# Giving ScalarE one row's sum of the first tile, in a kernel that divides rows by the sum of their absolute values

## Chip, cores, metric

One core of one Trainium2 chip. The metric is the device time of one execution in microseconds (us), median of the runs named. A span is the same execution as the trace sees it, 1.6 to 1.8 us shorter than the device time. VectorE and ScalarE are the two engines that compute here; SyncE only issues transfers. The DMA engines do the copying between the chip's main memory and the tile buffers, and take their work from queues. Tiles and loads are counted from 0.

## The reference

```python
# x: (32, 512, 1024) float32
sums = np.sum(np.abs(x), axis=-1, keepdims=True)
return (x / (sums + 1e-8)).astype(np.float32)
```

That is 16384 rows of 1024 numbers: 67.1 MB are read and as many written, in float32, and nothing in the problem allows less.

## The kernel before

The rows are cut into eleven tiles: ten of 128 partitions x 12 rows (6.29 MB each), and a last one of 8 rows (4.19 MB). Four buffers hold tiles. For each tile SyncE issues the load, VectorE sums the absolute values of all rows, adds epsilon and takes the reciprocal, VectorE and ScalarE share the multiplication by rows, and ScalarE's queue issues the store. The load of tile i+4 has to wait until the store of tile i has landed, because they share a buffer.

```python
R = 12; BUFS = 4
... # rows = [12]*10 + [8]; piece(flat, i) is the part of x or out of tile i
def normalize(x_tile, r0, k, kv):
    s = stats.tile([P, R], FP32)
    nc.vector.tensor_reduce(out=s[:, :k], in_=x_tile[:, r0 : r0 + k, :],
        axis=mybir.AxisListType.X, op=mybir.AluOpType.add, apply_absolute_value=True)
    nc.vector.tensor_scalar_add(out=s[:, :k], in0=s[:, :k], scalar1=EPS)
    inv = stats.tile([P, R], FP32)
    nc.vector.reciprocal(out=inv[:, :k], in_=s[:, :k])
    nc.vector.tensor_mul(out=x_tile[:, r0 : r0 + kv, :], ...)        # kv rows on VectorE
    for r in range(kv, k):                                           # the rest on ScalarE
        nc.scalar.activation(out=row, in_=row, func=...Copy, scale=inv[:, r : r + 1])

for i, k in enumerate(rows):
    x_tile = sbuf.tile([P, R, d], FP32)
    nc.sync.dma_start(out=x_tile[:, :k, :], in_=piece(x_flat, i))
    normalize(x_tile, 0, k, k - k // 3 - (i == 0))
    nc.scalar.dma_start(out=piece(out_flat, i), in_=x_tile[:, :k, :])
```

## Time and profile before

| | before |
|---|---|
| device time, 3 runs | 317.16 us (316.67 to 318.14) |
| span of the profiled run | 315.5 us |
| moved by DMA | 134.2 MB, 425 GB/s over the span |
| VectorE, ScalarE busy | 74%, 15% of the span |
| last load used from, last store issued | 280.36 us, 296.24 us |

How to read it: at the steady rate of 434 GB/s (the prediction shows the row) the bytes alone need 134.2 / 0.434 = 309.2 us of the 315.5. The table says at once that VectorE is the busiest compute engine.

### The profile page before, as it was taken

How to read it: one execution, taken by the hardware profiler on the slowest of the kernel's cores; microseconds unless marked ns; L12 is line 12 of the kernel's file. 1: busy time of each engine (PE TensorE's matmuls, PEld its weight loads, DVE VectorE, ACT ScalarE, POOL GpSimd, SP SyncE). 2: the span in 40 equal slices, each digit the busy share in tenths (PEclk: the TensorE clock that was granted, in tenths of full speed). 3: DMA queues.
4: the chain of work that ended last, by engine and by line, in shares of the span. 5: the costliest groups of instructions: out<-in, count | busy, mean ns of one | idle time of the engine just before them, and what ended most of it. 6: DMA issues, size and time to landing. Idle time of an engine off the chain costs nothing.

```text
span 315.5 us, 206 instructions
## 1 busy us (share of the span) xinstructions
DVE 234.7 (74%) x44; ACT 47.2 (15%) x44; POOL 0.2 (0%) x4
## 2 busy tenths in 40 slices
DVE  0079999999999399929955992899199659979500
ACT  0010603105005001300500050013004000502000
POOL 0000000000000000000000000000000000000000
DMA  8999999999999999999999999999999999999996
GB/s 330 467 399 430 467 343 455 399 467 430 399 467 430 399 486 411 405 486 405 424 474 399 436 461 399 467 430 399 467 425 405 474 403 459 407 472 411 424 432 274
DMA packets 3169, 134.23 MB, mean 425 GB/s; under 512 B 352, under 2 KB 352, under 8 KB 352
## 3 DMA queue, kind: packets, MB, share of 16 engines
q1 hardware_dynamic: 1584, 67.11, 49.8%
q10 hardware_dynamic: 1584, 67.11, 49.1%
q14 instruction: 1, 0.01, 0.0%
HBM read 67.11 MB, written 67.11 MB: 425 GB/s over the span
## 4 chain that ended last, share of the span: by engine, by line
another core or an unknown queue 36%; DMA 31%; DVE 26%; SPq 0%; issue 0%; DVEq 0%; ACTq 0%
DMA x_tile<-in_x_dram 16%; DMA out_dram<-x_tile 15%; DVE s L51 15%; DVE x_tile L61 10%; SPq L78 0%; DVE inv L60 0%; DVE s L58 0%; DVEq L60 0%; ACTq L81 0%
## 5 line engine op out<-in xcount | busy, mean ns | idle before, releaser
L51 DVE TENSOR_REDUCE s<-x_tile 128x12 f32<-128x12288 f32 (+1 forms) x11 | 138.2, 12563 | 59.8 <-DMA x_tile<-in_x_dram 59.8
L61 DVE TENSOR_TENSOR x_tile<-x_tile,inv 128x8192 f32<-128x8192 f32 (+2 forms) x11 | 92.4, 8401 | 0.4
L68 ACT ACTIVATE x_tile<-x_tile,inv 128x1024 f32<-128x1024 f32 x43 | 45.9, 1136 | 226.9 <-DVE inv L60 226.9
L68 ACT ACT_TABLE_LOAD x1 | 1.3, 1283 | 17.7 <-DMA x_tile<-in_x_dram 17.7
L60 DVE RECIPROCAL inv<-s 128x12 f32<-128x12 f32 (+1 forms) x11 | 2.5, 226 | 0.9
L58 DVE TENSOR_SCALAR s<-s 128x12 f32<-128x12 f32 (+1 forms) x11 | 1.9, 173 | 0.4
L96 POOL MEMSET const-bfloat16-1.0<- 128x1 bf16 x1 | 0.1, 102 | 0.0
L96 POOL MEMSET const-uint8-127<- 128x1 uint8 x1 | 0.1, 102 | 0.0
L96 POOL MEMSET const-float32-0.0<- 128x1 f32 x1 | 0.1, 99 | 0.2 <-issue 0.2
L96 POOL MEMSET const-float32-1.0<- 128x1 f32 x1 | 0.1, 99 | 0.0
## 6 DMA issues: line engine op xcount, KB each, us to landing
x_tile<-in_x_dram SPq DMA_DIRECT2D x10, 6144.0 KB, 37.6
out_dram<-x_tile ACTq DMA_DIRECT2D x10, 6144.0 KB, 50.7
x_tile<-in_x_dram SPq DMA_DIRECT2D x1, 4096.0 KB, 32.3
out_dram<-x_tile ACTq DMA_DIRECT2D x1, 4096.0 KB, 18.2
```

The source lines that it names most:

```text
L51: nc.vector.tensor_reduce(out=s[:, :k], in_=x_tile[:, r0 : r0 + k, :], axis=mybir.AxisListType.X, op=mybir.AluOpType.add, apply_absolute_v ...
L58: nc.vector.tensor_scalar_add(out=s[:, :k], in0=s[:, :k], scalar1=EPS)
L60: nc.vector.reciprocal(out=inv[:, :k], in_=s[:, :k])
L61: nc.vector.tensor_mul(out=x_tile[:, r0 : r0 + kv, :], in0=x_tile[:, r0 : r0 + kv, :], in1=inv[:, :kv].unsqueeze(2).to_broadcast([P, kv, d]),)
L68: nc.scalar.activation(out=row, in_=row, func=mybir.ActivationFunctionType.Copy, scale=inv[:, r : r + 1],)
L96: nc = _bacc.Bacc("TRN2", target_bir_lowering=False, num_devices=1)
```

## The change

Its intent: shorten the way to the first store. Until the first tile is done, ScalarE has nothing to do, so it takes over the sum of one of the twelve rows (absolute value with an accumulated sum; the elementwise result goes to a scratch tile in PSUM, another memory on the chip, that nobody reads).

```diff
+    junk = psum.tile([P, d], FP32)
-    def normalize(x_tile, r0, k, kv):
+    def normalize(x_tile, k, ks, kv):
         nc.vector.tensor_reduce(
-            out=s[:, :k],
-            in_=x_tile[:, r0 : r0 + k, :],
+            out=s[:, :ks],
+            in_=x_tile[:, :ks, :],
             ...
+        for r in range(ks, k):
+            nc.scalar.activation(
+                out=junk[:, :],
+                in_=x_tile[:, r, :],
+                func=mybir.ActivationFunctionType.Abs,
+                accum_out=s[:, r : r + 1],
+            )
         ...
-            normalize(x_tile, 0, k, k - k // 3 - (i == 0))
+            if i == 0:
+                normalize(x_tile, k, k - 1, k - 5)
+            else:
+                normalize(x_tile, k, k, k - k // 3)
```

Cut: the creation of the PSUM pool, and index changes where r0, always 0, falls away.

More of the change, by code (lines that the diff above doesn't have):

```diff
@@ L46 @@
     stats = ctx.enter_context(tc.tile_pool(name="stats", bufs=4))
-    def normalize(x_tile, r0, k, kv):
+    psum = ctx.enter_context(
+        tc.tile_pool(name="psum", bufs=1, space=bass.MemoryType.PSUM)
+    )
+    junk = psum.tile([P, d], FP32)
+    def normalize(x_tile, k, ks, kv):
         s = stats.tile([P, R], FP32)
         nc.vector.tensor_reduce(
-            out=s[:, :k],
-            in_=x_tile[:, r0 : r0 + k, :],
+            out=s[:, :ks],
+            in_=x_tile[:, :ks, :],
             axis=mybir.AxisListType.X,
@@ L57, in normalize @@
         )
+        for r in range(ks, k):
[4 more added lines that the diff above has]
+                accum_out=s[:, r : r + 1],
+            )
         nc.vector.tensor_scalar_add(out=s[:, :k], in0=s[:, :k], scalar1=EPS)
@@ L61, in normalize @@
         nc.vector.tensor_mul(
-            out=x_tile[:, r0 : r0 + kv, :],
-            in0=x_tile[:, r0 : r0 + kv, :],
+            out=x_tile[:, :kv, :],
+            in0=x_tile[:, :kv, :],
             in1=inv[:, :kv].unsqueeze(2).to_broadcast([P, kv, d]),
@@ L66, in normalize @@
         for r in range(kv, k):
-            row = x_tile[:, r0 + r, :]
+            row = x_tile[:, r, :]
             nc.scalar.activation(
```

## The prediction

> **What bounds the kernel now.** I read the slices of the page first, then the windows table cut at the changes of stage, then the waits of VectorE, and last the timeline of the first tile, because that is where the edit is.
>
> ```profile
> DMA  8999999999999999999999999999999999999996
> HBM read 67.11 MB, written 67.11 MB: 425 GB/s over the span
> ```
>
> The DMA engines are at 90% or more in 38 of 40 slices; only the first and the last have room. VectorE is busy for 74% and ScalarE for 15%. So the question is not how busy VectorE is but whether the DMA queues ever run dry because VectorE is late. The windows table answers by stage (columns: stretch, its length, busy time of VectorE, ScalarE and GpSimd, granted clock, DMA share, GB/s):
>
> ```profile
> 4.00:38.80 34.80, 21.04 (x5) 6.59 (x6) 0.00 (x0) 1.00 1.01 436
> 38.80:80.00 41.20, 40.99 (x8) 8.53 (x8) 0.00 (x0) 1.00 1.02 427
> 80.00:110.00 30.00, 24.82 (x5) 4.27 (x4) 0.00 (x0) 1.00 0.99 428
> 110.00:139.00 29.00, 22.05 (x4) 4.26 (x4) 0.00 (x0) 1.00 1.00 434
> 280.30:296.20 15.90, 15.62 (x4) 2.19 (x2) 0.00 (x0) 1.00 0.96 417
> 296.20:313.50 17.30, 0.00 (x0) 0.00 (x0) 0.00 (x0) 1.00 0.95 410
> ```
>
> From 4.0 to 38.8 us there are loads alone, then loads and stores together, and after 280.3 us (the last load has landed) stores alone. Loads alone already move 436 GB/s, the mixture 427 to 434, stores alone 410 to 417. A steady tile is 29.00 us long, which is 2 x 6.29 MB at 434 GB/s, while VectorE needs 22.05 us of it. In the query of the queues between 110 and 255 us the load queue and the store queue hold 50.1% each: when both have work they share equally, some 217 GB/s each.
>
> VectorE's waits say when it is ahead of the transfers and when behind:
>
> ```profile
> DVE s L51 <- DMA x_tile<-in_x_dram: 59.8, 8, 17.7
> ```
>
> Eight of eleven reduces waited for their load: the first (17.7 us), then none until the fifth tile (6.3 us), and some 6.8 us in each tile after. Tiles 1 to 3 run back to back on VectorE, from 38.66 to 105 us, and there alone could time saved on VectorE move anything. The edit is in the tile before them:
>
> ```profile
> 17.66 12.95 DVE L51 TENSOR_REDUCE s<-x_tile 128x12 f32<-128x12288 f32 x1 [17.66 <-DMA x_tile<-in_x_dram]
> 17.71 1.28 ACT L68 ACT_TABLE_LOAD   x1 [17.71 <-DMA x_tile<-in_x_dram]
> 30.65 0.18 DVE L58 TENSOR_SCALAR s<-s 128x12 f32<-128x12 f32 x1
> 30.86 0.23 DVE L60 RECIPROCAL inv<-s 128x12 f32<-128x12 f32 x1
> 31.12 5.30 ACT L68 ACTIVATE x_tile<-x_tile,inv 128x1024 f32<-128x1024 f32 x5 [12.13 <-DVE inv L60]
> 31.12 7.62 DVE L61 TENSOR_TENSOR x_tile<-x_tile,inv 128x7168 f32<-128x7168 f32 x1
> 38.66 12.94 DVE L51 TENSOR_REDUCE s<-x_tile 128x12 f32<-128x12288 f32 x1
> 38.83 0.37 ACTq L81 DMA_DIRECT2D out_dram<-x_tile  x1
> ```
>
> ScalarE loads its table at 17.71, is done at 18.99 and then stands idle for 12.13 us until the reciprocal. That hole is where the change puts its sum.
>
> **What the Trainium skill says.** "Perfetto Trace Analysis", section Roofline, gives about 435 GB/s as what one core's 16 DMA engines can pull together. The 434 GB/s of the steady stretch agrees: there is nothing left to win in it. "DMA: Bandwidth & Descriptors", section Queues, rings and completion order, says each DMA engine goes round robin, packet by packet, between the queues with work; the 50.1% and 50.1% agree. "ScalarE: Activation LUTs", section Table sets: the hidden batching unit, lists cheap functions such as copy and abs as filler in every set, so abs followed by copy should need one table load, and section What ACT_TABLE_LOAD costs puts the load at about 1283 ns; the trace has one of 1.28 us. Whether abs shares copy's set no trace of the kernel before can show.
>
> **The change, part by part.** Only tile 0 differs. The argument list loses an offset that was always 0. The split of the multiplication stays: before, 12 - 4 - 1 = 7 rows on VectorE and 5 on ScalarE; after, k - 5 = 7 and 5.
>
> Removed: one row of VectorE's first reduce. A reduce of 12 rows takes 12.95 us and of 8 rows 8.69 us, so a row is (12.95 - 8.69) / 4 = 1.065 us and the fixed part 0.17 us. Eleven rows come to 0.17 + 11 x 1.065 = 11.88 us, 1.07 us less. If it starts at 17.66 as before, it ends at 29.54 rather than 30.61.
>
> Added: one 128x1024 ScalarE activation with abs, and the output of its accumulator. The 128x1024 activations here have a mean of 1.136 us; with a short second instruction for the accumulator I estimate 1.1 to 1.4 us. It follows the table load, at 18.99, and ends near 20.4, some 9 us before VectorE is through its eleven rows. Both write parts of one statistics tile, and both read one data tile. The two multiplications of this kernel already write parts of one tile at the same time (both start at 31.12), so the dependence is kept by region and the two sums should not wait for each other. The unneeded output goes to a scratch tile in PSUM that nobody else uses.
>
> Added: a wait of VectorE's small addition for ScalarE's sum. It has long been met; where later tiles wait on a second engine, the gap between the small addition's start and the reciprocal's is 0.28 us (124.16 to 124.44) in place of 0.21 (30.65 to 30.86), so I allow 0.07 us.
>
> Sum on VectorE: 1.07 - 0.07 = 1.0 us earlier. The reciprocal begins near 29.8, the multiplication near 30.1, the second reduce near 37.6, and the first store is issued near 37.8 in place of 38.83.
>
> **What that does to the end.** The queue does not stand idle before that first store: loads 1 to 3 are still on their way at 436 GB/s. An earlier store therefore takes half the rate from the loads. In the 1.0 us by which it starts sooner the loads lose 1.0 x 217 GB/s = 0.22 MB, which costs them another 1.0 us at their half rate. So every store moves 1.0 us forward and every load 1.0 us back.
>
> The first load to matter is the fourth. It is issued near 2.3 us (the last of four that take from 0.73 to 2.65) and takes the longest time to landing of any, 80.1 us, so it lands near 82.4; VectorE gets to it at 82.78, with 0.4 us to spare. After the change VectorE is there near 81.8 and the load near 83.4. The saving ends there: tile 3 should show a new wait of about 1.6 us and begin some 0.6 us later than before. From then on VectorE waits for loads in every tile, as before.
>
> At the end: the last load lands near 281.4 in place of 280.34, the last reduce, multiplication and store follow with the same 15.9 us, and the last store is issued near 297.2 in place of 296.24. Has it room? Before, 17.3 us of stores alone at 410 GB/s are 7.1 MB, of which the last store is 4.19 MB, so 2.9 MB or 7.1 us of older stores lay in front of it. Losing 1.0 us of these 7 leaves the queue full. The end is when all 134.2 MB have been moved. What remains is a change of mixture: the stretch with stores alone gets about 1 us shorter and is 4 to 5% slower than the mixed one (413 against 434), which is worth 0.05 us. The predicted time is 317.16 - 0.05, say 317.1 us.
>
> **The rivals.** *The gain comes through whole:* a microsecond on the only back-to-back stretch of VectorE, carried to the end, would give 316.1 us. For it speaks that the chain of waits runs through VectorE from 17.66 to 82.89 us. Against it, the chain then passes into transfers of a queue that never empties, and the fourth load has only 0.4 us of slack. Even this is 0.3%.
>
> *The sums wait for each other:* if the shared statistics tile makes ScalarE's sum follow VectorE's reduce, tile 0 takes about 0.2 us more than before (1.2 added, 1.07 saved, a further hand-over) and the time is still 317.2. The simultaneous writes at 31.12 speak against it.
>
> *A second table load:* if abs and copy lie in different sets, 1.28 us come either into the idle hole (free) or between the reciprocal and the five copies; these would end at 1.28 + 5.30 = 6.6 us, still before VectorE's 7.62. Nothing is lost: 317.1.
>
> *The order of transfers:* stores begin earlier and meet other packets; the stretch 38.8 to 110 us runs at 427 to 428 GB/s, 1.5% below the steady 434, so about 71 x 0.015 = 1.1 us is lost there. A different phase could win back or double a part of it: 316.5 to 317.9. This is the only way I see to a shift above noise, and I can't tell its sign.
>
> **Range and chances.** All rivals lie between 316.1 and 317.9. The three runs of before lie between 316.67 and 318.14, so the median of a few runs has about half a microsecond of noise of its own. I take 316.2 to 318.0 for 8 in 10. A shift of 2% is 6.3 us, more than everything this change touches, so I give 98% to the same time and 1% to either side; these are for a surprise in the DMA rate.
>
> **What would show it.** Right: a first reduce of 128x11264 taking 11.9 us; an activation into the junk tile between 19 and 21 us, beside it; one table load; the first store near 37.8; a wait of VectorE for a load before the fourth reduce, which was not there; later reduces about 1 us later than before, the last store issued near 297; 434 GB/s in the steady tiles. Wrong: if later reduces start 1 us earlier and the end too (the loads didn't pay for the store), if ScalarE's sum starts after the reduce has ended, or if the steady tile is no longer 29.0 us.

## The result, and the profile after

317.25 us (317.09 to 317.71, 6 runs) against 317.32 us (316.67 to 318.14, 6 runs). The ratio is 0.9997 with a 95% interval of [0.9982, 1.0013]: the same. Here and below a ratio is the mean time of one kernel's fast runs over the mean of the other's fast runs of the same rounds, so it is not quite the ratio of the medians quoted.

The timeline of the first tile after the change (start us, length us, engine, line, operation; in brackets the idle time before and what ended it):

```profile
0.72 1.28 ACT L65 ACT_TABLE_LOAD   x1 [0.72 <-PEq L112]
...
17.75 1.03 ACT L65 ACTIVATE junk<-x_tile 128x1024 f32<-128x1024 f32 x1 [15.75 <-DMA x_tile<-in_x_dram]
17.75 11.89 DVE L57 TENSOR_REDUCE s<-x_tile 128x11 f32<-128x11264 f32 x1 [17.75 <-DMA x_tile<-in_x_dram]
18.72 0.19 ACT L65 ACTIVATION_READ_ACCUMULATOR junk<-x_tile 128x1 f32 x1
29.75 0.17 DVE L71 TENSOR_SCALAR s<-s 128x12 f32<-128x12 f32 x1
29.96 0.23 DVE L73 RECIPROCAL inv<-s 128x12 f32<-128x12 f32 x1
30.22 7.63 DVE L74 TENSOR_TENSOR x_tile<-x_tile,inv 128x7168 f32<-128x7168 f32 x1
...
37.77 12.95 DVE L57 TENSOR_REDUCE s<-x_tile 128x12 f32<-128x12288 f32 x1
37.94 0.37 ACTq L97 DMA_DIRECT2D out_dram<-x_tile  x1
```

The edit does what it was made for. ScalarE's sum lies wholly beside VectorE's shorter reduce, and the first store is issued at 37.94 us in place of 38.83. Further lines of the timelines show where this ends: at the fourth reduce. Before, then after:

```profile
82.78 12.95 DVE L51 TENSOR_REDUCE s<-x_tile 128x12 f32<-128x12288 f32 x1
```

```profile
82.05 0.34 ACTq L97 DMA_DIRECT2D out_dram<-x_tile  x1
82.77 12.95 DVE L57 TENSOR_REDUCE s<-x_tile 128x12 f32<-128x12288 f32 x1 [0.80 <-DMA x_tile<-in_x_dram]
```

The fourth reduce began at 82.78 before; it begins at 82.77 now, after a new wait of 0.80 us for its load. VectorE had finished the tile before it 0.9 us sooner (at 81.96 in place of 82.86) and stood idle for nearly all of that. VectorE's waits in total, after:

```profile
DVE s L57 <- DMA x_tile<-in_x_dram: 61.8, 9, 17.8
```

Nine waits in place of eight, and 61.8 us in place of 59.8. The 2.0 us more are about the 1.06 us of work that was taken away and the 1.06 us by which, as the next lines show, the last reduce begins later. And at the other end of the kernel, first before, then after:

```profile
280.36 8.69 DVE L51 TENSOR_REDUCE s<-x_tile 128x8 f32<-128x8192 f32 x1 [1.96 <-DMA x_tile<-in_x_dram]
...
296.24 0.34 ACTq L81 DMA_DIRECT2D out_dram<-x_tile  x1
```

```profile
281.42 8.69 DVE L57 TENSOR_REDUCE s<-x_tile 128x8 f32<-128x8192 f32 x1 [1.96 <-DMA x_tile<-in_x_dram]
...
297.29 0.34 ACTq L97 DMA_DIRECT2D out_dram<-x_tile  x1
```

The first store moved 0.89 us forward, and the last load and the last store moved 1.06 and 1.05 us BACK, while the device time stayed. This is what a fixed rate shared by two queues would look like: what the stores get sooner, the loads get later. One pair of traces does not prove it, however. The slower last tile, below, runs the program of before up to its last tile, and its last load was used at 280.75 us, 0.39 us later than in the trace of before. So some of the 1.06 us may be the run and not the change; the five-row kernel, below, shows the same shift at 4.4 us.

### The profile page after: what moved, and what is told of

Its sections match the earlier page's. It is cut to its first block, busy times and chain, and to the rows that moved or that the text cites. A ratio compares the mean times of both kernels' runs of the same rounds, so it can differ in the third digit from the quotient of the medians.

```text
span 315.9 us, 208 instructions
## 1 busy us (share of the span) xinstructions
DVE 233.8 (74%) x44; ACT 48.3 (15%) x46; POOL 0.2 (0%) x4
## 4 chain that ended last, share of the span: by engine, by line
another core or an unknown queue 36%; DMA 32%; DVE 25%; SPq 0%; issue 0%; DVEq 0%; ACTq 0%
DMA x_tile<-in_x_dram 16%; DMA out_dram<-x_tile 15%; DVE s L57 15%; DVE x_tile L74 10%; SPq L91 0%; DVE inv L73 0%; DVE s L71 0%; DVEq L73 0%; DVEq L71 0%; ACTq L97 0%
## 5 line engine op out<-in xcount | busy, mean ns | idle before, releaser
L57 DVE TENSOR_REDUCE s<-x_tile 128x12 f32<-128x12288 f32 (+2 forms) x11 | 137.1, 12467 | 61.8 <-DMA x_tile<-in_x_dram 61.8
L65 ACT ACTIVATE junk<-x_tile 128x1024 f32<-128x1024 f32 x1 | 1.0, 1027 | 15.7 <-DMA x_tile<-in_x_dram 15.7
```

What stands on the lines that cost most here:

```text
L57: nc.vector.tensor_reduce(out=s[:, :ks], in_=x_tile[:, :ks, :], axis=mybir.AxisListType.X, op=mybir.AluOpType.add, apply_absolute_value=True,)
L65: nc.scalar.activation(out=junk[:, :], in_=x_tile[:, r, :], func=mybir.ActivationFunctionType.Abs, accum_out=s[:, r : r + 1],)
```

## The experiments

Theory: the end is pinned by the bytes; a head start of VectorE in the first tile only shifts turns between the load and the store queue. Rivals: (A) the head start is carried to the end but one microsecond is lost in noise; (B) the new sum costs as much as it saves; (C) some computing elsewhere is on the path, and only the place of the edit was wrong. Rival B needs no run of its own: the trace above has the sum beside the reduce, and the store 0.89 us sooner. All of these ran with correct results unless said otherwise.

**Five rows instead of one.** From the changed kernel:

```diff
-                normalize(x_tile, k, k - 1, k - 5)
+                normalize(x_tile, k, k - 5, k - 5)
```

> ScalarE sums five rows of tile 0 and VectorE seven. Theory (an earlier store is paid for by the loads, the end is pinned by the bytes): the first reduce takes 0.17 + 7 x 1.065 = 7.6 us, ScalarE's five sums some 5.5 us beside it, the first store is issued near 33.7 us (5.2 us before that of the kernel before), the last reduce starts 5.2 us LATER than before, near 285.5, the last store near 301.4, time 317.0 us, within 0.5 us of before. The room before the last store shrinks from 7 to about 2 us but stays positive. Rival (a head start of VectorE is carried to the end, one microsecond was only lost in noise): 5 us off, 312 us, and the last reduce starts near 275.

318.01 us (317.45 to 320.95, 6 runs) against 317.50 (11 runs); ratio 1.0021 [0.9977, 1.0066]. The timeline of its first store, of the third and fourth reduces and of its end:

```profile
33.63 0.38 ACTq L97 DMA_DIRECT2D out_dram<-x_tile  x1
...
57.25 12.95 DVE L57 TENSOR_REDUCE s<-x_tile 128x12 f32<-128x12288 f32 x1 [1.65 <-DMA x_tile<-in_x_dram]
86.26 12.95 DVE L57 TENSOR_REDUCE s<-x_tile 128x12 f32<-128x12288 f32 x1 [6.86 <-DMA x_tile<-in_x_dram]
...
284.79 8.69 DVE L57 TENSOR_REDUCE s<-x_tile 128x8 f32<-128x8192 f32 x1 [1.94 <-DMA x_tile<-in_x_dram]
...
300.67 0.34 ACTq L97 DMA_DIRECT2D out_dram<-x_tile  x1
```

The first store leaves 5.2 us sooner than in the kernel before (33.63 against 38.83), the fourth reduce begins 3.5 us LATER (86.26 against 82.78) and the last 4.4 us later; I had expected 5.2. The time does not fall. Rival A wanted 312 us and falls.

**A slower first tile.** The kernel before, with one more reduce of the tile in tile 0, its result unused:

```diff
+        for _ in range(extra):                     # extra = 1 for tile 0, else 0
+            t = spare.tile([P, R], FP32)
+            nc.vector.tensor_reduce(out=t[:, :k], in_=x_tile[:, r0 : r0 + k, :], ...)
```

> The kernel before with one more reduce of 12 rows (12.95 us) in tile 0, its result unused. Theory: the stores start 13 us later, near 51.8, the loads get ahead; the store queue is never empty afterwards, so the DMA engines stay full; the last reduce starts EARLIER than before, between 267 and 276 us; the stretch with stores alone gets longer and is 4 to 5% slower, worth 0.3 to 0.7 us; time 317.2 to 318.2 us. Rival (the chain of waits through VectorE in the first 83 us sets the end): 330 us. Rival (half of it shows): about 323.

319.91 us median, but its runs are wide: 317.35 to 324.69, two of six slow; ratio of the fast runs 1.004 [0.999, 1.009]. Against the 13 us added this is nothing or at most about 3 us; the interval can't say whether the small loss is real. The profiled run, at 317.35, is the fastest of the six, and its span is 315.6 us against 315.5; its trace can't say what the slower runs lost. The windows table of this run shows that in it the DMA engines did not notice (same columns as in the prediction):

```profile
38.80:80.00 41.20, 40.99 (x9) 9.57 (x9) 0.00 (x0) 1.00 1.01 422
80.00:110.00 30.00, 29.79 (x8) 5.26 (x5) 0.00 (x0) 1.00 1.00 429
110.00:139.00 29.00, 28.82 (x5) 7.53 (x8) 0.00 (x0) 1.00 1.00 434
```

VectorE is busy without a gap here (29.79 of 30 us), and the rates are within 1.2% of those of the kernel before, 427, 428 and 434. My number for the last reduce was wrong: I said 267 to 276 us, it began at 279.25, only 1.1 us earlier than before. The queues say why. Between 66 and 80 us of this run:

```profile
q10 hardware_dynamic: 138, 6.00, 99.0%
q1 hardware_dynamic: 16, 0.00, 0.1%
```

The load queue (q1) moved nothing: all four buffers were full, and the next load could be issued only when the first store had landed, at 77.18 us. Meanwhile the stores (q10) had the engines to themselves, at 428 GB/s, and made up what they had lost. The load of tile 5 is then issued at 102.55 us, against 102.58 in the kernel before. So the lead of the loads over the stores is capped by the buffers, and a delay of 13 us is forgotten within two tiles.

**A slower last tile.** The same extra reduce, twice, in the last tile instead (extra = 2 for tile 10).

> The kernel before with two more reduces of 8 rows (17.4 us) in the LAST tile, results unused. Theory: older stores hide about 7 us of it, the rest shows: last store issued near 313.6, time 317.2 + 17.4 - 7.1 = 327.5 us (326.5 to 328.5). Rival (VectorE is nowhere on the path, as the busy shares suggest): 317. Rival (the tail has no room at all): 334.6.

328.60 us (328.32 to 329.25, 4 runs); ratio 1.0346 [1.0301, 1.0392], slower, 11.1 us over the median of before and 1.1 us above my point, just outside the range I gave. The windows table of the end:

```profile
296.20:303.00 6.80, 6.80 (x2) 0.00 (x0) 0.00 (x0) 1.00 1.05 455
303.00:313.60 10.60, 10.43 (x4) 2.19 (x2) 0.00 (x0) 1.00 0.01 5
313.60:325.00 11.40, 0.12 (x1) 0.00 (x0) 0.00 (x0) 1.00 0.86 369
```

This is what it looks like when VectorE is on the path: at 303 us the older stores are through, and the engines stand at 5 GB/s for 10.6 us until the last store is issued at 313.81. The last store came 313.81 - 296.24 = 17.6 us later and the span grew by 326.8 - 315.5 = 11.3 us, so older stores hid 6.3 us; I had worked out 7.1. So it is the place of the work, and not the share of busy time, that decides whether it shows: 13 us added in the first tile showed next to nothing, 17.4 us in the last showed 11.

**No computing at all.** WRONG ON PURPOSE: the call of normalize is left out, tiles are stored as loaded.

```diff
-            normalize(x_tile, 0, k, k - k // 3 - (i == 0))
```

> WRONG ON PURPOSE: the tiles are stored as they were loaded, no computing at all, same tiles, buffers and queues. Theory (bytes pin the time): about 2 us of start, 134.2 MB at about 434 GB/s, about 2 us to land the last store, and a shorter stretch of stores alone: 315 to 317 us, so all the computing costs about 1 us. Rival (computing on the path, which a better split could win back by more than 2%): under 311 us.

316.99 us (316.60 to 317.86, 6 runs) against 317.50; ratio 0.9982 [0.9942, 1.0022]. The page of this run:

```profile
span 315.2 us, 80 instructions
...
DMA  8989999999999999999999999999999999999997
```

A copy through the same tiles takes as long as the kernel, within the interval. In the two profiled runs all computing together costs 0.3 us of span (315.5 against 315.2), less than the spans of the copy differ among themselves (314.8 to 316.1). With this, rival C falls too: as far as the copy is the floor, no other split of the work between the engines can win more than the interval leaves, 0.6%, with these tiles and queues. That the copy is the floor is argued: it moves the same bytes, but in another order in time, its first store being issued at 17.63 us.

**Small pieces at both ends.** A try for a version that beats both: pieces of 4, ten times 12, and 4 rows; VectorE sums all. From the changed kernel; cut: the bounds of the pieces, and the call for tile 0, which becomes `normalize(x_tile, k, k, k - 1)`.

```diff
-    HEAD = 32
+    HEAD = 8
-    rows = [R] * ((per_partition - HEAD) // R + 2) + [HEAD - 2 * R]
+    rows = [HEAD // 2] + [R] * ((per_partition - HEAD) // R) + [HEAD // 2]
```

> Pieces of 4, ten times 12, and 4 rows in place of 12 (ten times) and 8; VectorE sums all. The first store can be issued near 15 us, so the loads lead by 13 us in place of 36 and the stretch with stores alone shrinks from 33 us to about 15. Theory: only the 4 to 5% slower rate of stores alone can be won back, 18 us x 0.045 = 0.8 us: 316.5 us, not below the copy without computing (317.0) by more than its noise, so 316.0 to 317.5. Rival (the long stretches of one direction are a real loss of several us, which an earlier first store would cure): 312 to 314. Rival (so small a lead lets a queue run dry): over 319, with waits in the profile.

317.72 us (317.04 to 317.89, 6 runs) against 317.55; ratio 0.9995 [0.9960, 1.0029]. The first store is issued at 16.31 us, 22.5 us sooner than before, and nothing comes of it. The expected 0.8 us did not appear either; from 15 to 60 us, when stores had joined the loads, this kernel moved only 417 GB/s, and from 298 to 314 us only 379. So what the mixture could give was lost there or was never there; no run separates the two.

**Three buffers.** Does the same hold when buffers are scarce? The kernel before, the changed kernel and the five-row kernel, each with `BUFS = 3`, the first two in two sessions.

> The kernel before with three buffers in place of four. A load is issued when the store of the tile three before it has landed. Theory: the load queue runs dry for some us in each tile while stores keep the engines busy, 318 to 326 us; DMA share mostly still 0.9 or more.

> The changed kernel with three buffers. Theory: as the kernel before with three buffers, within 1 us (first store 0.9 to 1.0 us earlier, not carried to the end, as the transfers bind still). Rival (it is the fourth buffer that swallowed the microsecond): 1 us faster than the three-buffer kernel before, with every reduce 1 us earlier to the last.

> The kernel before with three buffers, a second time, as the partner of the next two: 330 to 333 us in its fast runs.

> The changed kernel with three buffers, a second time, since three of its four runs were slow. If the microsecond is carried through with three buffers, its profile shows later reduces about 1.2 us earlier than those of the three-buffer kernel before, as in the first pair, and its fast runs are about 1 us shorter; if that was chance, the sign differs this time.

> Five rows summed by ScalarE in tile 0, three buffers: first store 5.1 us earlier. If three buffers let a head start through: the last reduce about 5 us earlier, and about 326 us. If the bytes bind here too: the time of the three-buffer kernel before within 1.5 us.

| three buffers | all runs, us | fast runs of these | ratio to the four-buffer kernel before |
|---|---|---|---|
| before, first session | 330.39 to 335.33 | 4 of 4 | 1.0469 [1.0398, 1.0540] |
| changed, first session | 330.28 to 338.51 | 1 of 4 | none |
| before, second session | 324.31 to 337.88 | 1 of 6 | none |
| changed, second session | 330.53 to 337.67 | 5 of 6 | 1.0481 [1.0417, 1.0545] |
| five rows, second session | 328.70 to 336.10 | 5 of 6 | 1.0427 [1.0365, 1.0489] |

Two things follow. Three buffers cost about 4 to 5%, more than the 318 to 326 us that I had expected: the reduces wait for loads by up to 14 us. And the comparison is not settled. In the first session's profiled runs every later reduce of the changed kernel is 1.1 to 2.5 us earlier (the last at 300.24 against 301.52) and the span is 1.3 us shorter (328.1 against 329.4), which would suit the rival that the fourth buffer swallows the microsecond. But runs of one and the same three-buffer kernel differ by 5 to 14 us, and a run is marked slow when it is over 1.5% above the fastest of its kernel, so one lucky run (324.31) turns all the others slow. In the second session the profiled runs of two of the three kernels were slow, so I compare no traces there. The ratios of the changed and the five-row kernel overlap with that of the kernel before. With three buffers the question whether a head start is carried through stays open.

## Why the prediction was right

**The time and the bound.** Predicted 317.1 us, measured 317.25. The 0.05 us that the mixture was to give is far below the noise and is not shown. "There is nothing left to win" in the steady stretch was the load-bearing step. The steady tiles still move 434 GB/s after the change, and the copy without computing takes 316.99 us, the kernel's time within the interval. One line was misread on the way: the waits after the fifth tile are not all some 6.8 us, the last was 1.96 us. Nothing rests on it.

**The price of the sum.** Predicted 11.88 us for the reduce of eleven rows, measured 11.89; predicted 1.1 to 1.4 us for ScalarE's sum, measured 1.03 + 0.19 with a small overlap. The two sums did not wait for each other, and there was one table load, so abs and copy did share a set. One step had the wrong place: I put the sum after the table load, at 18.99 us. The table load began at 0.72 us, where the kernel before had it wait for the tile (why it no longer waits, the trace does not show), and the sum began with the reduce at 17.75. It changed nothing, since ScalarE's sum ended over 10 us before VectorE's.

**The first store.** Predicted 37.8 us, measured 37.94. The difference is that the first tile's load was used 0.09 us later than before. The 0.07 us allowed for the second wait came as predicted, but before the small addition (0.11 us after the reduce's end in place of 0.04), not after it.

**The loads pay.** Predicted: every store about 1.0 us sooner and every load about 1.0 us later, with a last reduce near 281.4 and a last store near 297.2. Measured: 281.42 and 297.29. The direction is right, and the five rows confirm it. That the last reduce agrees to less than a tenth is in part luck, since two traces of what is up to there the same program differ by 0.39 us, and the steps on the way were not 1.0. The load of tile 4 waits for the first store to land; its issue, before, then after:

```profile
73.52 0.33 SPq L78 DMA_DIRECT2D x_tile<-in_x_dram  x1
```

```profile
71.75 0.33 SPq L91 DMA_DIRECT2D x_tile<-in_x_dram  x1
```

So the first store landed 1.8 us sooner. The fourth load took 80.6 us to landing in place of 80.1, only 0.5 us longer, so the fourth reduce waited 0.80 us and not the predicted 1.6. The next ones began 0.59 us later (111.76 against 111.17), then 0.82, 0.82, 1.22, 1.09, 1.06 and 1.06.

The term that was mis-sized is the exchange at the first store. The working had the store take half of the rate as soon as it is issued. But in both kernels the store queue moved nothing before 43 us, with the store issued at 38.83 us before and at 37.94 after. From 43 to 73 us the two queues shared equally in the kernel before:

```profile
q1 hardware_dynamic: 149, 6.54, 51.2%
q10 hardware_dynamic: 150, 6.64, 51.1%
```

After the change the stores had more in the same stretch, 6.93 MB against 6.29 MB of loads. So the earlier issue did not bring the store's first bytes forward; it got the stores a larger part of what followed. Why a store that is issued behind loads waits 4 us and more, and why the turns then fell as they did, no run here shows.

**The tail.** I took about 7 us of older stores as the room before the last store; the slower last tile measured 6.3. The change took 1.05 us of that room.

## What to carry to other kernels

When the DMA engines are full from the first load to the last store, time saved on a compute engine is first turned into idle time of that engine, and an earlier store is paid for by later loads; check the last load and the last store, not only the first. A kernel stripped of its computing gives an estimate of the floor in one run, and it should come before any rebalancing of engines. Where work can still matter is the stretch after the last load: there the room is what older stores leave in the queue, here 6 us, and of a delay of 17.6 us the other 11.3 showed.

## What the Trainium skill lacked or had wrong

- "DMA: Bandwidth & Descriptors", section Where 436 GB/s comes from, says that for transfers between HBM and SBUF the HBM side, about 358 GB/s, binds. Here one core moved 434 GB/s of such transfers for over 140 us on end, half loads and half stores. The same page's measured table (425 GB/s for 16 MB) and "Perfetto Trace Analysis", section Roofline (about 435 GB/s), fit the measurement.
- The same page, section Queues, rings and completion order, has each DMA engine go round robin between queues; no page says how long a store that is issued while loads fill the engines waits for its first turn. The store queue moved nothing before 43 us where the store was issued at 38.83 us (before) and at 37.94 us (after), and nothing before 39.5 us where it was issued at 33.63 us (five rows). Later the queues held 50.1% each.
- "ScalarE: Activation LUTs", section What ACT_TABLE_LOAD costs, gives 186 ns + 0.833 ns per element for an activation with immediate scale and bias, and 93 ns for a pointer operand: 1039 and 1132 ns for 1024 elements. The runs show 1027 ns (abs into PSUM) and a median of 1132 ns (copy with a pointer scale), so these two hold within 1.2%. No page gives the price of the accumulator's output on ScalarE: a second instruction of 186 ns, and 1.18 us from one such sum to the next (17.71 to 18.89 in the five-row kernel).
- The same page, section Step-by-step: what each stage is for, has the table load right before the activation that needs it. Whether the load waits for that activation's tile differs, and no page says so: it began at 17.71 us, with the landing of the tile, in the kernel before, and at 0.72 us in the changed one.
